# Layer 1's modulation vectors: from TensorE filler matmuls to VectorE sums inside the two-stream MLP

## The chip, the cores and the metric

One core of a Trainium2 chip runs the whole program. The metric is the device time of one execution in microseconds (us), the median of several executions. The engines are TensorE (PE), VectorE (DVE), ScalarE (ACT), GpSimd (POOL) and SyncE (SP, which issues nearly all DMA transfers here). The profile comes from one profiled execution.

## The reference, cut to what matters

A 256 x 1024 fp32 tensor passes through a first block (a hybrid layer and a recurrent layer, each with a squared-ReLU MLP) and then a second block of two layers on two streams, the tokens `xl` and a context `xc`. In each of its two layers, six modulation vectors per stream shift, scale and gate the normalised activations:

```python
def modulation(cvec, w_mod, b_mod):
    m = jax.nn.silu(cvec) @ w_mod + b_mod
    return jnp.split(m[:, None, :], N_MOD, axis=-1)      # N_MOD = 6

for i in range(DEPTH):                                   # DEPTH = 2
    ml = modulation(c, w_mod[i], b_mod[i])
    mc = modulation(c_ctx[None, :], w_mod[i], b_mod[i])
    hl = modulate(rmsnorm(xl, g_pre_mix[i]), ml[0], ml[1])
    hc = modulate(rmsnorm(xc, g_pre_mix[i]), mc[0], mc[1])
    ...
    xl_new = xl + ml[2] * rmsnorm(y_l, g_post_mix[i])
    h2 = modulate(rmsnorm(xl_new, g_pre_mlp[i]), ml[3], ml[4])
    xl_new = xl_new + ml[5] * rmsnorm(sqrelu_mlp_2(h2, w_mlp_in[i], w_mlp_out[i]), g_post_mlp[i])
```

`w_mod[i]` is 1024 x 6144 in fp32, 24 MB a layer, and both streams' vectors come from the same product, of a 2 x 1024 matrix with it. The vectors depend on `c` and `c_ctx` alone, so they can be made at any time before their layer uses them.

## The kernel before, in words

Order of the program, with the times of the trace: the hybrid layer (to 216 us), its MLP (to 402), the recurrent layer (to 515), its MLP (to 695), the second block's layer 0 on both streams (to about 950), the MLP of both streams, `mlp512` (to 1294), layer 1 (to 1440), and the last MLP. Nearly all matmuls hold fp32 accuracy by a split of each operand into a high and a low part. A weight unit of 1 MB is loaded into one of two buffers `wr`; ACT casts each half to `wh` (L407) and DVE subtracts to get `wl` (L408), four buffers each; every product is then three matmuls (high by high, high by low, low by high, L342). `pa`, `pb`, `pc` and `pm` are PSUM tiles: four banks, two, one and one.

The modulation vectors are made by the generator `mods()`: 48 steps, 24 for each of the two layers of the second block. A layer's 24 are three groups q of eight steps k. A step takes two tiles `wm` of 512 KB (four buffers, loaded on SP's queue at L737) and issues four fp32 matmuls (L776): the stationary operand is `cs_t[:, k, :]`, 32 columns of which two are used, the moving one 512 columns of `wm`, and the four write the four groups of 32 columns of one bank `pm`, a sum over k. After the eighth step DVE adds the bias and applies the gains (L782, L783), and `cols_of` turns the result by four transposes into `pc`, which DVE copies to `mc` (L755). Each matmul appears in the trace as two records.

What sets their place: calls `fill(n)` in the other stages take steps from the generator, and a scheduler fixes the order of the instructions on each engine ahead of the run; `tc.high_priority(-10)` marks these matmuls as to be placed late, as filler. The steps of layer 0 end at about 402 us. Those of layer 1 lie at 402 to 478, 694 to 780, 949 to 953 and 1299 to 1350 us.

In `mlp512` a unit of the first weight makes 256 hidden columns for each of the streams (`up`, into `pb`, squared ReLU by ACT and DVE at L560 and L1937), a unit of the second one is summed into four tiles of outputs (`acc`, into `pa`, added by DVE at L1948). Two `up` units and two `acc` units alternate. The last of the steps (two calls, j >= 14) were asked for here.

Of the kernel before, what the change touches and what calls it, by code (L numbers as in the profile page):

```python
# [10 lines left out]
F32 = mybir.dt.float32  # L11
# [4 lines left out]
P = 128  # L16
# [1 line left out]
SM = 1.0 / math.sqrt(96.0)  # L18
NW = 4
LEAD = 96  # L20
TRAIL = 24
ALPHA = 4.0 ** 0.25

ADD, SUB, MUL, MAX, MIN, POW = ALU.add, ALU.subtract, ALU.mult, ALU.max, ALU.min, ALU.pow
# [269 lines left out]
def hybrid_then_mla(ctx: ExitStack, tc: tile.TileContext, a, out, usizes):  # L294
    nc = tc.nc
# [18 lines left out]
    def s4(shape, dt=F32):  # L314
        return tmp.tile(shape, dt, tag="s4", bufs=5, name=nm("s4"))
# [19 lines left out]
    def psM():  # L335
        return psp.tile([P, 512], F32, tag="pm", bufs=1, name=nm("pm"))
# [4 lines left out]
    def mm(o, l, r, start, stop):  # L341
        T.matmul(o, l, r, start=start, stop=stop)  # L342
# [99 lines left out]
    half = cpool.tile([P, 8], F32, name="half")  # L442
    V.memset(half, -0.5)

    def row(name, n=1024, o=0):
        r = tmp.tile([P, 1024], F32, tag="row", bufs=3, name=nm("row"))
        i = ROWS.index(name)
        nc.sync.dma_start(out=r[:, :n], in_=a["rows"][i : i + 1, o : o + n].to_broadcast([P, n]))
        return r
# [273 lines left out]
        V.tensor_tensor(c2, c2, th, op=MUL)  # L723

    class WM:
        tiles, n = {}, 0

    def mod_load():

        if WM.n >= 48:  # L730
            return
        i, q, k = WM.n // 24, WM.n // 8 % 3, WM.n % 8
        for j in range(2):
            wm = wpool.tile([P, 2, 512], F32, tag="wm", bufs=4, name=nm("wm"))
            if WM.n < 2:
                G.tensor_copy(wm[:, 0, 0:1], WM.after)
            nc.sync.dma_start(out=wm, in_=a["wm"][i, q, k, j].rearrange("p (a b) -> p a b", a=2))  # L737
            WM.tiles[WM.n, j] = wm
        WM.n += 1

    mc = cpool.tile([P, 2, 3, 32], F32, name="mc")
    cpool.tile([P, TRAIL], F32, name="trail")

# [5 lines left out]
    def mods():  # L749

        def cols_of(m, i, q):
            pt = psC()
            for c in range(4):
                tr(pt[:, 128 * c : 128 * c + 128], m[:, 128 * c : 128 * c + 128])
            V.tensor_copy(mc[:, i, q].rearrange("p (c r s) -> p c r s", c=4, r=4),  # L755
                          pt.rearrange("p (c r s) -> p c r s", c=4, r=4)[:, :, :, 0:2])

        todo = None
        for n in range(48):
            i, q, k = n // 24, n // 8 % 3, n % 8  # L760
            if k == 0:
                ps = psM()
            if k == 1 and todo:
                cols_of(*todo)
            if k == 4:
                bg = s4([P, 2, 512])
                for r in range(4):
                    nc.sync.dma_start(
                        out=bg[32 * r : 32 * r + 32],
                        in_=a["bg"][i, q, r : r + 1].rearrange("o (a b) -> o a b", a=2).to_broadcast([32, 2, 512]),  # L770
                    )
            while WM.n < min(n + 2, 48):
                mod_load()
            for r in range(4):
                with tc.high_priority(-10):
                    mm(ps[32 * r : 32 * r + 32, :], cs_t[:, k, :], WM.tiles[n, r // 2][:, r % 2, :], k == 0, k == 7)  # L776
            mod_load()
            if k < 7:
                yield
                continue  # L780
            m = s2([P, 512])
            V.tensor_tensor(m, ps, bg[:, 0, :], op=ADD)  # L782
            V.scalar_tensor_tensor(m, m, K("one")[:, q : q + 1], bg[:, 1, :], op0=ADD, op1=MUL)  # L783
            for r in range(4):
                if 2 * q + r // 2 in (2, 5):
                    nc.sync.dma_start(
                        out=mdr[i, :, 2 * q + r // 2, 512 * (r % 2) : 512 * (r % 2) + 512], in_=m[32 * r : 32 * r + 2]
                    )
            todo = (m, i, q)
            yield  # L790
        cols_of(*todo)
        yield

    mod_g = mods()

    def fill(n):
        _take(mod_g, n)

    def run(g):
        for _ in g:  # L800
# [1065 lines left out]
    def layer1(xs, Ts, late):  # L1866

        m = Mixer(1)
        m.Ts = Ts
        w = (w_next(8), w_next(8))  # L1870
        fill(2)
        run(conf_inputs(m, w, 0))
        cg = conf_conv(m)
        late(0)
        w = (w_next(4), w_next(4))
        x0, x1 = latents(m, 1, 0, w), latents(m, 1, 1, w)
        _take(x0, 2)
        _take(x1, 2)
        _take(cg, 1)
        run(x0)  # L1880
        late(1)
        c0, c1 = latents(m, 0, 0, w, 160), latents(m, 0, 1, w, 160)
        _take(c0, 2)
        run(x1)
        fill(1)
        _take(cg, 1)
        _take(c1, 2)
        run(c0)
        run(c1)
        fill(1)  # L1890
        del m.Ts[0]
        gbr = row("g_branch1")
        cgb = row("conf1", 512)
        wq, wk = w_next(2), w_next(1)
        run(chain(queries(m, 1, wq), keys_values(m, 0, wk), keys_values(m, 1, wk)))
        m.qkT.clear()
        sc = short_conv(m)
        side = zipped(cg, sc, 2)
        at = attend(m, 1, 0)
        _pace(at, side, 1)  # L1900
        run(side)
        mc = lambda t: merge_conv(m, 1, t, gbr, cgb)
        ma = lambda t: merge_attn(m, 1, t, gbr)
        side = pipelined(mc(0), mc(1), ma(0))
        at = attend(m, 1, 1)
        _take(at, 2)
        _pace(at, side, 1)
        run(side)
        run(ma(1))
        fill(99)  # L1910
        GP = mrow(1, 0, 2)
        nT = Late()

        def done(t, halves):
            post_norm(xs[1][t], halves, GP)
            y = normed(xs[1][t])
            nT.fn[t] = lambda: to_xT(y, t, nT.xT, mod=(1, 1, 4))

        tm1024(m.mT[1], done, nT, (2, 3, 0, 1))
        return nT  # L1920

    def mlp512(Ts, xs, late):
# [27 lines left out]
        for kind, j in _mlp_order_512():  # L1950
            if kind == "w1":
                if j == 0:
                    w = (w_next(8), w_next(8))
                    q = {}
                    for i in range(2):
                        hid[i] = b8([P, 2, 2, 512], F32R)

                    def hid_tr(n):
                        p3 = head_tr(q[n])
                        sl = (slice(None), slice(None), slice(128 * n, 128 * n + 128))  # L1960
                        for i in range(2):
                            split(p3[:, 2 * i : 2 * i + 2], hid[i][:, 0][sl], hid[i][:, 1][sl])

                    before = None
                    for n in (2, 3, 0, 1):
                        late(n)
                        q[n] = square_relu(head(Ts[n // 2], n % 2, w))
                        if before is not None:
                            hid_tr(before)
                        before = n  # L1970
                elif j > 1:
                    w = w_next(8)
                    for s in (1, 0):
                        up(j, w, s)
                        if j == 2 and s:
                            hid_tr(1)
                    if j >= 14:
                        fill(1)
            elif j < 7:
                for c in range(2):  # L1980
                    w = w_next(4)
                    for n in range(4):
                        acc(j, c, w, n)
                del hid[2 * j], hid[2 * j + 1]
            else:
                GP = [mrow(0, 1, 5), mrow(0, 0, 5)]
                wa, wb = w_next(4), w_next(4)
                T1 = {1: new_xT()}
                fn = {}

                def ready(n):
                    if n in fn:
                        fn.pop(n)()

                def done(n):
                    s, t = n // 2, n % 2
                    y = yacc[n]
                    post_norm(xs[s][t], [y[:, 0:512], y[:, 512:1024]], GP[s])
                    z = normed(xs[s][t])

                    def go():
                        if s not in T1:
                            T1[s] = new_xT()
                        to_xT(z, t, T1[s], mod=(1, s, 1))

                    fn[n] = go

                for n in (2, 3):
                    acc(j, 0, wa, n)
                    acc(j, 1, wb, n)  # L2010
                    done(n)
                acc(j, 0, wa, 0)
                acc(j, 1, wb, 0)
                ready(2)
                acc(j, 0, wa, 1)
                ready(3)
                acc(j, 1, wb, 1)
                done(0)
                done(1)
# [47 lines left out]
```

## Time and profile before

| | us |
|---|---|
| median of 3 executions | 1632.86 (1632.76 to 1634.14) |
| the profiled execution | 1635.88 |
| its span in the trace | 1633.8 |
| PE busy | 1578.0 (97%) |
| DVE busy | 1029.0 (63%) |
| ACT busy | 743.3 (45%) |
| all `pm` matmuls of modulation, busy | 83.2 |

The span is 2.1 us short of the profiled execution's time, and that execution is 3.0 us above the median. A busy share is an average over stages with different limits: where an engine is busy all the time, an instruction added to it costs its full duration, and where it waits for others, an instruction removed from it may give nothing.

### The profile page before, as it was taken

How to read it: one execution, taken by the hardware profiler on the slowest of the kernel's cores; microseconds unless marked ns; L12 is line 12 of the kernel's file. 1: busy time of each engine (PE TensorE's matmuls, PEld its weight loads, DVE VectorE, ACT ScalarE, POOL GpSimd, SP SyncE). 2: the span in 40 equal slices, each digit the busy share in tenths (PEclk: the TensorE clock that was granted, in tenths of full speed). 3: DMA queues.
4: the chain of work that ended last, by engine and by line, in shares of the span. 5: the costliest groups of instructions: out<-in, count | busy, mean ns of one | idle time of the engine just before them, and what ended most of it. 6: DMA issues, size and time to landing. Idle time of an engine off the chain costs nothing.

```text
span 1633.8 us, 24905 instructions
## 1 busy us (share of the span) xinstructions
PE 1578.0 (97%) x10182; PEld 1358.9 (83%) x10182; DVE 1029.0 (63%) x1593; ACT 743.3 (45%) x1264; POOL 94.8 (6%) x121
## 2 busy tenths in 40 slices
PE   7999999999999999999999999999999999989998
PEld 7866679888878998877877789999999788779997
DVE  6874575556787556768974753444444789775555
ACT  5642244443574445436454543222222475554443
POOL 0021000000000000003010100000000030000000
PEclk9999999999999999999999999999999999989999
DMA  7865475555665554562310432222232262235553
GB/s 289 288 217 172 167 258 196 204 207 191 248 258 181 194 192 169 181 227 80 130 52 27 138 134 89 93 103 85 97 104 79 100 216 107 73 126 201 181 186 124
DMA packets 46946, 259.77 MB, mean 159 GB/s; under 512 B 5600, under 2 KB 5856, under 8 KB 24304
## 3 DMA queue, kind: packets, MB, share of 16 engines
q1 hardware_dynamic: 46832, 258.18, 44.9%
q8 instruction: 80, 1.31, 0.3%
q14 instruction: 34, 0.28, 0.1%
HBM read 257.08 MB, written 1.08 MB: 158 GB/s over the span
## 4 chain that ended last, share of the span: by engine, by line
PE 78%; DVE 8%; ACT 4%; DMA 2%; POOL 1%; issue 1%; POOLq 0%; DVEq 0%; ACTq 0%; SPq 0%
PE pa L342 44%; PE pb L342 27%; PE pm L342 4%; PE pb L366 2%; DVE wl L408 1%; DMA wr<-in_wp_dram 1%; PE pc L366 1%; ACT s L1389 1%; ACT wh L407 1%; DVE s L1583 1%; POOL ti L1395 1%; ACT s L1652 0%; DVE s L645 0%; DVE b L711 0%; DVE xt L1426 0%
## 5 line engine op out<-in xcount | busy, mean ns | idle before, releaser
L408 DVE TENSOR_TENSOR wl<-wr,wh 128x1024 fp32r<-128x1024 f32 (+2 forms) x366 | 443.4, 1217 | 301.4 <-ACT wh L407 288.4
L407 ACT CAST wh<-wr 128x1024 fp32r<-128x1024 f32 (+2 forms) x364 | 376.1, 1041 | 405.8 <-PE pa L342 202.6
L342 PE MATMUL pa<-wh,b 128*128 128x512 f32 (+3 forms) x1456 | 411.1, 365 | 12.5 <-ACT b L816 5.7
L342 PE MATMUL pb<-b,wh 128*128 128x256 f32 x2240 | 406.2, 284 | 0.0
L342 PEld LDWEIGHTS pb<-b,wh 128*128 128x128 f32 x2240 | 352.7, 192 | 7.2 <-issue 3.4
L342 PE MATMUL pb<-b,wl 128*128 128x256 f32 x1120 | 317.8, 284 | 0.0
L342 PEld LDWEIGHTS pa<-wh,b 128*128 128x128 f32 x1456 | 267.6, 195 | 57.1 <-ACT b L648 6.1
L342 PE MATMUL pa<-wl,b 128*128 128x512 f32 (+3 forms) x728 | 258.7, 364 | 8.9 <-DVE wl L408 8.9
L342 PE MATMUL pa<-wh,s 128*128 128x512 f32 x768 | 244.5, 391 | 0.0
L342 PEld LDWEIGHTS pb<-b,wl 128*128 128x128 f32 x1120 | 215.1, 192 | 1.7 <-issue 1.7
L342 PE MATMUL pa<-b,wh 128*128 128x256 f32 x1056 | 199.2, 289 | 3.7 <-ACT wh L407 1.9
L342 PEld LDWEIGHTS pa<-b,wh 128*128 128x128 f32 x1056 | 166.2, 193 | 16.0 <-issue 4.4
L342 PEld LDWEIGHTS pa<-wl,b 128*128 128x128 f32 x728 | 142.3, 195 | 35.3 <-DVE wl L408 13.5
L342 PEld LDWEIGHTS pa<-wh,s 128*128 128x128 f32 x768 | 144.4, 188 | 28.9
L342 PE MATMUL pa<-b,wl 128*128 128x256 f32 x528 | 150.1, 288 | 1.3 <-DVE wl L408 1.3
L342 PE MATMUL pa<-wl,s 128*128 128x512 f32 x384 | 150.4, 392 | 0.0
L342 PEld LDWEIGHTS pa<-b,wl 128*128 128x128 f32 x528 | 101.6, 193 | 8.2 <-DVE wl L408 3.3
L560 DVE TENSOR_TENSOR s<-s 128x512 f32<-128x512 f32 x80 | 54.9, 687 | 50.2 <-ACT s L558 50.2
L342 PE MATMUL pm<-wm,cs_t 128*32 128x512 f32 x384 | 83.2, 606 | 1.9 <-DMA wm<-in_wm_dram 1.7
L342 PEld LDWEIGHTS pa<-wl,s 128*128 128x128 f32 x384 | 72.3, 188 | 14.5 <-DVE wl L408 1.2
L1583 DVE SCALAR_TENSOR_TENSOR s<-cu,cols_sb,s 128x512 f32<-128x512 f32 (+1 forms) x120 | 70.7, 621 | 0.5
L366 PE MATMUL pb<-kc_sb,s 128*128 128x128 f32 x366 | 56.8, 279 | 10.8 <-DVE s L1408 2.5
(278 smaller groups left out, 1391.6 us busy)
## 6 DMA issues: line engine op xcount, KB each, us to landing
wr<-in_wp_dram SPq DMA_DIRECT2D x176, 1024.0 KB, 4.8
wm<-in_wm_dram SPq DMA_DIRECT2D x96, 512.0 KB, 5.2
row<-in_rows_dram SPq DMA_DIRECT2D x10, 512.0 KB, 5.5
wr<-in_wp_dram SPq DMA_DIRECT2D x4, 832.0 KB
s<-in_bg_dram SPq DMA_DIRECT2D x24, 128.0 KB, 5.6
row<-mdr SPq DMA_DIRECT2D x6, 512.0 KB, 3.5
wr<-in_wp_dram SPq DMA_DIRECT2D x4, 264.0 KB, 3.6
b<-in_xT_dram SPq DMA_DIRECT2D x4, 256.0 KB, 6.1
```

The costliest lines, as they stand in the source:

```text
L342: T.matmul(o, l, r, start=start, stop=stop)
L366: T.transpose(o, i, ident)
L407: S.copy(h[:, :n], r)
L408: V.tensor_tensor(l[:, :n], r, f(h[:, :n]), op=SUB)
L560: V.tensor_tensor(q, r, r, op=MUL)
L1389: S.activation(j, x, AF.Square, scale=scale, accum_out=o)
L1395: G.tensor_tensor(r, e, half[:, :1], op=POW)
L1583: V.scalar_tensor_tensor(ac, src, w(k), ac, op0=MUL, op1=ADD)
```

## The change

The steps of layer 0 stay in place. For layer 1, DVE takes over the sum over k: for each of three q and two halves j, two tiles `acc[0]` and `acc[1]` of 128 x 1024 (one for each stream; they take the three `row` buffers) collect `wm * c` over eight k, the first by TENSOR_SCALAR (L819), the seven others by SCALAR_TENSOR_TENSOR (L821), with the scalar a column of `cs_t`. What is left is a sum over the 128 partitions, which PE does with a stationary tile `sel` that has ones in one column and zeros in the rest: four matmuls for each (q, j), two column groups of `pm` with two matmuls each. Together that is 96 DVE operations (12 and 84) and 24 matmuls in place of the 96 matmuls of layer 1. Bias, gains and `cols_of` follow for each q. A new `fill1()` takes these units: after each `up` with j > 2, and after every second `acc` of the units with e < 7, all in `mlp512`. `fill` stops at the end of layer 0's steps. The loads of `wm` for layer 1 move along on SP's queue.

```diff
@@ mods(), layer 1
+        for q in range(3):
+            ps = psM()
+            for j in range(2):
+                acc = [row_tile() for _ in range(2)]
+                for k in range(8):
+                    n = 48 + 16 * q + 8 * j + k
+                    mod_load(n + 3)
+                    w = WM.tiles.pop((1, q, k, j)).rearrange("p a b -> p (a b)")
+                    for s_ in range(2):
+                        c = cs_t[:, k, s_ : s_ + 1]
+                        with tc.high_priority(-10):
+                            if k == 0:
+                                V.tensor_scalar(acc[s_], w, c, None, op0=MUL)
+                            else:
+                                V.scalar_tensor_tensor(acc[s_], w, c, acc[s_], op0=MUL, op1=ADD)
+                    mod_load(n + 4)
+                    yield
+                for r in (2 * j, 2 * j + 1):
+                    with tc.high_priority(-10):
+                        for s_ in range(2):
+                            mm(ps[32 * r : 32 * r + 32, :], sel[:, s_, :], acc[s_][:, 512 * (r % 2) : 512 * (r % 2) + 512], s_ == 0, s_ == 1)
+            cols_of(*biased(ps, gains(1, q), 1, q))
+            yield
@@ mlp512
                     for s in (1, 0):
                         up(j, w, s)
+                        if j > 2:
+                            fill1()
...
-                    if j >= 14:
-                        fill(1)
...
                     for n in range(4):
                         acc(j, c, w, n)
+                        if n % 2:
+                            fill1()
```

On PE, where the first products of the second block's layer 0 begin after the recurrent layer's MLP (about 698 us), the order before has this run of filler. `b`, `wh` and `wl` are operands of the products, the `pc` row is the transposes of `cols_of`:

```order
L342 MATMUL pa_6621<-b_572_6024,wh_6553 128x256
L342 MATMUL pa_6621<-b_573_6025,wh_6553 128x256
L342 MATMUL pm_6673<-wm_5820,cs_t 32x512
L342 MATMUL pm_6673<-wm_5822,cs_t 32x512 x2
L342 MATMUL pm_6673<-wm_6198,cs_t 32x512 x2
L342 MATMUL pm_6673<-wm_6200,cs_t 32x512 x2
L366 MATMUL pc_6682<-kc_sb,s_596_6202 128x128 x4
L342 MATMUL pm_6673<-wm_6678,cs_t 32x512 x2
L342 MATMUL pm_6673<-wm_6680,cs_t 32x512 x2
L342 MATMUL pa_6571<-b_572_6024,wl_6550 128x256
```

In the order of the change the `pm` rows and the four `pc` transposes of `cols_of` are gone from here, and the `pa` rows follow each other.

On PE inside an `acc` unit of `mlp512`, where there was no `pm` row before, the change has six such groups of four matmuls. The first, the third and the fifth look like this (`row_9231` and `row_9232` are the two streams' sums):

```order
L342 MATMUL pa_9647<-wh_9601,b_1057_9351 128x512
L342 MATMUL pm_9230<-row_9231,sel 32x512
L342 MATMUL pa_9647<-wh_9601,b_1057_9351 128x512
L342 MATMUL pm_9230<-row_9232,sel 32x512
L342 MATMUL pm_9230<-row_9231,sel 32x512
L342 MATMUL pa_9647<-wl_9602,b_1057_9351 128x512
L342 MATMUL pm_9230<-row_9232,sel 32x512
L342 MATMUL pa_9647<-wh_9601,b_1057_9351 128x512
```

The second has one `pa` row after its first row, the fourth and the sixth are four rows together; all now stand between products that had followed each other without a break.

On DVE at the passage from layer 0 to `mlp512`, the order before has, from the second residual tile `xt_90` to its normalisation:

```order
L1426 SCALAR_TENSOR_TENSOR xt_90<-s_1004_8724,ti_8730,xt_90 128x512
L1394 SCALAR_TENSOR_TENSOR ti_8740<-ti_8736 128x1
L1408 TENSOR_SCALAR s_1009_8737<-xt_90,ti_8741 128x512 x2
L408 TENSOR_TENSOR wl_8598<-wr_8591,wh_8597 128x1024
L645 TENSOR_SCALAR s_1016_8785<-pb_8780,mc 128x128 x3
```

and the change has (its lines are 44 numbers further down, so L1470 is L1426, L1438 is L1394, L1452 is L1408):

```order
L1470 SCALAR_TENSOR_TENSOR xt_90<-s_972_8603,ti_8609,xt_90 128x512
L819 TENSOR_SCALAR row_9232<-wm_3048,cs_t 128x1024
L821 SCALAR_TENSOR_TENSOR row_9232<-wm_3050,cs_t,row_9232 128x1024
L1438 SCALAR_TENSOR_TENSOR ti_8619<-ti_8615 128x1
L408 TENSOR_TENSOR wl_8490<-wr_8483,wh_8489 128x1024
L1452 TENSOR_SCALAR s_977_8616<-xt_90,ti_8620 128x512 x2
L408 TENSOR_TENSOR wl_8780<-wr_8483,wh_8779 128x1024
```

Two of the sums, and a `wl`, have moved ahead of the normalisation.

## Rows read from the trace of the kernel before

**Rows 1.** The page, its span, busy time of engines, chain by line

```profile
span 1633.8 us, 24905 instructions
...
PE 1578.0 (97%) x10182; PEld 1358.9 (83%) x10182; DVE 1029.0 (63%) x1593; ACT 743.3 (45%) x1264; POOL 94.8 (6%) x121
...
PE pa L342 44%; PE pb L342 27%; PE pm L342 4%; PE pb L366 2%; DVE wl L408 1%; DMA wr<-in_wp_dram 1%; PE pc L366 1%; ACT s L1389 1%; ACT wh L407 1%; DVE s L1583 1%; POOL ti L1395 1%; ACT s L1652 0%; DVE s L645 0%; DVE b L711 0%; DVE xt L1426 0%
```

**Rows 2.** Windows by stage: PE, PEld, DVE, ACT, POOL busy, clock, DMA share, GB/s

```profile
402.00:480.00 78.00, 75.63 (x573) 63.62 (x572) 63.90 (x99) 51.57 (x85) 0.92 (x1) 1.00 0.65 242
...
1090.00:1140.00 50.00, 50.00 (x333) 46.24 (x333) 22.13 (x26) 15.57 (x19) 0.00 (x0) 1.00 0.25 85
...
1290.00:1350.00 60.00, 55.24 (x376) 44.89 (x374) 53.44 (x116) 41.17 (x88) 16.82 (x24) 1.00 0.52 178
```

**Rows 3.** Windows, instructions of tile pm alone: PE, PEld, DVE busy, clock, DMA, GB/s

```profile
402.00:480.00 78.00, 12.26 (x64) 1.96 (x64) 0.00 (x0) 1.00 0.65 242
694.00:780.00 86.00, 12.87 (x64) 2.11 (x64) 0.00 (x0) 0.98 0.43 154
...
sum 224.00, PE 36.30 PEld 5.91 DVE 0.00; mean PE 9.07 PEld 1.48 DVE 0.00
```

**Rows 4.** Chain of waits, 400 to 412 us: start, duration, what, records

```profile
by line: PE pa L342 50.1%; PE pm L342 39.7%; PE pc L366 8.5%; PE pb L366 3.6%
...
402.07 1.83 PE pm L342 x10
...
404.81 0.97 PE pm L342 x2
```

**Rows 5.** Chain of waits, 694 to 722 us

```profile
by line: PE pa L342 57.0%; DMA wm<-in_wm_dram 15.1%; PE pm L342 11.0%; DVE s L645 3.8%; PE pb L366 3.7%; ACT b L648 2.2%; DVE cu L1537 2.1%; ACT s L647 1.7%; PE pc L366 1.6%; SPq L737 1.0%; issue 0.9%; ACTq L647 0.1%
...
699.54 4.22 DMA wm<-in_wm_dram
...
703.80 1.05 PE pm L342 x4
```

**Rows 6.** Timeline of DVE at 410, 702 and 894 us: start, busy, what [idle before]

```profile
410.44 0.19 DVE L755 COPY mc<-pc 128x32 f32<-128x32 f32 x1 [1.89 <-PE pc L366]
...
701.63 1.17 DVE L408 TENSOR_TENSOR wl<-wr,wh 128x1024 fp32r<-128x1024 f32 x1
...
894.17 0.69 DVE L1421 TENSOR_TENSOR s<-s,row 128x512 f32<-128x512 f32 x1 [8.43 <-ACT s L1828]
```

**Rows 7.** Chain of waits, 432 to 484 us

```profile
by line: DMA wr<-in_wp_dram 22.2%; DVE wl L408 16.0%; DVE b L1365 9.1%; issue 6.5%; PE pa L342 4.9%; DVE b L1363 4.7%; DVE b L711 4.5%; ACT wh L407 4.1%; ACT b L1360 3.9%; DVE b L1269 3.5%; DVE b L1357 3.5%; ACT L1360 2.5%; DVE s L1319 2.4%
```

**Rows 8.** Chain of waits, 750 to 782 us

```profile
by line: PE pa L342 27.8%; issue 14.9%; ACT b L1498 9.2%; PE pm L342 8.8%; DVE b L1608 6.6%; DVE s L1607 6.5%; POOL s L1484 3.7%; ACT b L1621 3.6%; ACT b L1620 3.6%; ACT s L1603 3.4%; ACT s L1627 3.4%; ACT b L1496 2.7%; POOL ti L1467 2.1%; 
```

**Rows 9.** Chain of waits, 947 to 954 us

```profile
by line: PE pm L342 40.3%; PE pa L342 33.5%; PE pb L366 20.9%; PE pc L366 6.2%
```

**Rows 10.** Chain of waits, 1296 to 1352 us

```profile
by line: PE pa L342 37.5%; DMA wr<-in_wp_dram 11.1%; PE pm L342 8.8%; DVE wl L408 5.4%; ACT wh L407 4.9%; ACT s L1389 4.0%; DVE s L645 3.1%; PE pb L366 2.9%; issue 2.8%; POOL s L1484 2.8%; POOL ti L1395 2.2%; PE pc L366 2.0%; POOL ti L1467 
...
1332.64 0.99 PE pm L342 x8
```

**Rows 11.** DVE groups, from the page and from the answer on line 1408

```profile
L408 DVE TENSOR_TENSOR wl<-wr,wh 128x1024 fp32r<-128x1024 f32 (+2 forms) x366 | 443.4, 1217 | 301.4 <-ACT wh L407 288.4
...
L1583 DVE SCALAR_TENSOR_TENSOR s<-cu,cols_sb,s 128x512 f32<-128x512 f32 (+1 forms) x120 | 70.7, 621 | 0.5
...
L1408 DVE TENSOR_SCALAR s<-xt,ti x16: 479/484/489, 696.2 to 1445.5; 128x512 f32<-128x512 f32 x16
```

**Rows 12.** Windows, PE alone: busy, clock, DMA share, GB/s

```profile
506.00:510.00 4.00, 1.62 (x14) 1.00 0.10 16
510.00:514.00 4.00, 4.00 (x24) 0.58 0.92 358
...
702.00:706.00 4.00, 3.25 (x18) 1.00 1.03 412
```

More of the change, by code (lines that the diff above doesn't have):

```diff
@@ L20 @@
 LEAD = 96
-TRAIL = 24
+TRAIL = 88
 ALPHA = 4.0 ** 0.25
@@ L443, in hybrid_then_mla, with row_tile @@
     V.memset(half, -0.5)
+    def row_tile():
+        return tmp.tile([P, 1024], F32, tag="row", bufs=3, name=nm("row"))
     def row(name, n=1024, o=0):
@@ L725, in hybrid_then_mla, with mod_load @@
     class WM:
[L726 to L733, printed above, removed]
+        tiles, n, first = {}, 0, False
+        order = [(0, q, k, j) for q in range(3) for k in range(8) for j in range(2)]
+        order += [(1, q, k, j) for q in range(3) for j in range(2) for k in range(8)]
+    def mod_load(upto):
+        for n in range(WM.n, min(upto, len(WM.order))):
+            at = WM.order[n]
             wm = wpool.tile([P, 2, 512], F32, tag="wm", bufs=4, name=nm("wm"))
-            if WM.n < 2:
+            if n < 4:
                 G.tensor_copy(wm[:, 0, 0:1], WM.after)
-            nc.sync.dma_start(out=wm, in_=a["wm"][i, q, k, j].rearrange("p (a b) -> p a b", a=2))
-            WM.tiles[WM.n, j] = wm
-        WM.n += 1
+            nc.sync.dma_start(out=wm, in_=a["wm"][at].rearrange("p (a b) -> p a b", a=2))
+            WM.tiles[at] = wm
+            WM.n = n + 1
+    sel = cpool.tile([P, 2, 32], F32, name="sel")
+    V.memset(sel, 0.0)
+    for s_ in range(2):
+        V.memset(sel[:, s_, s_ : s_ + 1], 1.0)
     mc = cpool.tile([P, 2, 3, 32], F32, name="mc")
@@ L756, in cols_of, with gains, biased @@
                           pt.rearrange("p (c r s) -> p c r s", c=4, r=4)[:, :, :, 0:2])
[L758 to L773, printed above, removed]
-            for r in range(4):
[L775 to L780, printed above, removed]
+        def gains(i, q):
+            bg = s4([P, 2, 512])
+            for r in range(4):
+                nc.sync.dma_start(
+                    out=bg[32 * r : 32 * r + 32],
+                    in_=a["bg"][i, q, r : r + 1].rearrange("o (a b) -> o a b", a=2).to_broadcast([32, 2, 512]),
+                )
+            return bg
+        def biased(ps, bg, i, q):
             m = s2([P, 512])
@@ L788, in mods, with fill1 @@
                     )
-            todo = (m, i, q)
+            return m, i, q
+        todo = None
+        for n in range(24):
+            q, k = n // 8, n % 8
+            if k == 0:
+                ps = psM()
+            if k == 1 and todo:
+                cols_of(*todo)
+            if k == 4:
+                bg = gains(0, q)
+            mod_load(2 * n + 4)
+            for r in range(4):
+                with tc.high_priority(-10):
+                    mm(ps[32 * r : 32 * r + 32, :], cs_t[:, k, :], WM.tiles[0, q, k, r // 2][:, r % 2, :], k == 0, k == 7)
+            mod_load(2 * n + 6)
+            if k < 7:
+                yield
+                continue
+            todo = biased(ps, bg, 0, q)
             yield
         cols_of(*todo)
-        yield
+        yield "first"
+        for q in range(3):
+            ps = psM()
+            for j in range(2):
[7 more added lines that the diff above has]
+                        with tc.high_priority(-10):
+                            if k == 0:
+                                V.tensor_scalar(acc[s_], w, c, None, op0=MUL)
[4 more added lines that the diff above has]
+                for r in (2 * j, 2 * j + 1):
+                    with tc.high_priority(-10):
+                        for s_ in range(2):
+                            mm(ps[32 * r : 32 * r + 32, :], sel[:, s_, :], acc[s_][:, 512 * (r % 2) : 512 * (r % 2) + 512], s_ == 0, s_ == 1)
+            cols_of(*biased(ps, gains(1, q), 1, q))
+            yield
     mod_g = mods()
     def fill(n):
-        _take(mod_g, n)
+        for _ in range(n):
+            if not WM.first:
+                WM.first = next(mod_g) == "first"
+    def fill1():
+        next(mod_g, None)
     def run(g):
@@ L1909, in layer1 @@
         run(ma(1))
-        fill(99)
+        assert next(mod_g, None) is None
         GP = mrow(1, 0, 2)
```

## The prediction

> **What bounds the kernel now.** I read the page first: PE is busy 97% of the span and holds most of the chain that ended last, pa and pb products alone 71%, while DVE is busy 63% [rows 1]. That invites the change: take work from PE, give it to DVE. But the share is an average, so I read the windows by stage next. In the two-stream MLP PE is busy 50.00 of 50 us and DVE only 22.13; just after it, from 1290 to 1350 us, DVE is busy 53.44 of 60 and PE 55.24 [rows 2]. What is added to PE inside the MLP has nothing to lie beside. Then I read where layer 1's modulation matmuls lie: the tile pm alone takes 12.26 us of 402 to 480 and 12.87 of 694 to 780, and the four stretches that hold all 24 steps give 36.30 us together [rows 3]. Last I read the chain of waits through these stretches, to see which of that time ends anything.
>
> The chain's shares, times the lengths of their windows, say what pm is worth there at the most. 400 to 412 us: 39.7% of 12, 4.8 us [rows 4]. 432 to 484 us: no share at all; weights' DMA, wl and the recurrence on DVE fill the chain [rows 7]. 694 to 722 us: 11.0% of 28, 3.1 us, and another 4.2 us in which PE waited for a wm transfer [rows 5]. 750 to 782 us: 8.8% of 32, 2.8 us [rows 8]. 947 to 954 us: 40.3% of 7, 2.8 us [rows 9]. 1296 to 1352 us: 8.8% of 56, 4.9 us [rows 10]. Sum: 22.6 us of the 36.3. That is a ceiling for the gain, since behind each piece another wait stands ready.
>
> **What is removed, stretch by stretch.**
> - 400 to 412 us. The pms hold up four transposes on PE, and DVE's copy from pc had waited 1.89 us for them [rows 6]; the normalisation behind the copy carries the chain on. Beyond that the next products wait for ACT's split. I take 1.9 us, ends 0 and 4.8.
> - 432 to 484 us. The pms fill holes that DVE, ACT and the DMA make [rows 7]. The wr transfers are 22.2% of 52 us, 11.5 us, and share the queues with wm; these loads go. I take 0.75 us, ends 0 and 3.
> - 694 to 722 us. The wait for wm and the pm behind it end at 703.80 + 1.05 = 704.85 us [rows 5]. The next product needs a wl that DVE finishes at 701.63 + 1.17 = 702.80 [rows 6]. So 2.0 us, ends 0 and 7.3, and PE then idles where it had filler.
> - 750 to 782 us. ACT, DVE and POOL hold the rest of that chain [rows 8] and will be late next. I take 1.2 us, ends 0 and 2.8.
> - 947 to 954 us. 2.8 us of pm go, but DVE gets new work in the passage before it: the order puts a TENSOR_SCALAR and a SCALAR_TENSOR_TENSOR of 128x1024, by the prices below 2.2 us, ahead of the normalisation of the second tile, on which transposes and then products wait. The four sums that are put earlier fall in a hole of 8.43 us on DVE [rows 6] and cost nothing; without that hole they would be some 5 us. I take a net gain of 0.5, ends 2.8 and a loss of 1.5.
> - 1296 to 1352 us. DVE is busy 89% there [rows 2] and its convolution paces the stretch, so of 4.9 us I take 0.75, ends 0 and 4.9.
>
> Sum of gains 1.9 + 0.75 + 2.0 + 1.2 + 0.5 + 0.75 = 7.1 us.
>
> **What the holes cost.** Where the filler goes, PE idles some us. From 506 to 510 us PE was busy 1.62 us of 4, and in the next 4 us its mean granted clock was 0.58, full speed being 2.4 GHz and the lower level half of it: 0.42 x 4 = 1.7 us lost. From 702 to 706 us, with a shorter hole, it stayed at 1.00 [rows 12]. New holes come at about 410, 700 and 1300 us. I take 2.0 us, a little over one such loss; ends 0 and 5.1 for three.
>
> **What is added to PE.** Twenty-four matmuls with 32 columns out and 512 in, in six groups of four, all inside products that keep PE at 50 of 50 us. Such a matmul alone (two records) takes 0.97 us of PE; a whole step of four, one for each column group, takes 0.99 (eight records) [rows 4, 10]; and ten records, a step and one matmul more, take 1.83 [rows 4]. So different column groups run side by side and a second matmul for the same group takes another 0.85 or so. A group of the change is s0, s1 of one column group, then s0, s1 of the next: the two middle ones can pair, so three rounds, 0.97 + 0.86 + 0.86 = 2.7 us where the four stand together, and 3 x 0.97 = 2.9 where products stand between them. Six of them: about 2.8 x 6 = 16.9 us. Lower end two rounds, 1.83 x 6 = 11.0; upper end no pairing, 4 x 0.97 x 6 = 23.3. The trace has no two matmuls of one column group that follow each other directly with others waiting, so I keep both ends.
>
> A page speaks of this: the Trainium skill, TensorEngine Tiling (Array Packing), section Theoretical Speedup, gives up to four times for operands of at most 32 columns, from independent 128x32 tiles. By it two column groups would run fully in parallel, which is the lower end, and the sum below would be 5.9 us smaller; the step of four in 0.99 us agrees with it, and no row shows it for two matmuls queued on each of two groups.
>
> Layer 1's three cols_of, of four transposes each, now stand in the full stretch too. Two sets of transposes hold 8.5% of 12 us of the chain from 400 us, 1.0 us [rows 4], so three are 1.5; they cost something where they stood before, and I take 1.3, ends 0 and 1.5.
>
> **What is added to DVE.** Twelve TENSOR_SCALAR and 84 SCALAR_TENSOR_TENSOR of 128x1024, neither in the trace at this size. Twice the 128x512 forms, 0.484 and 0.621 us [rows 11], is 0.97 and 1.24; L408, as large, takes 1.22. So 12 x 0.97 + 84 x 1.24 = 116 us over some 310 us, 37 points on top of 44% [rows 2]: 81%. DVE stays short of full; sums wait where wl and the y additions go first. I price it at 0 here, because wl is made ahead into four buffers, up to about 10 us where that cover fails. The loads, 24 MB over 310 us, add 77 GB/s to the 85 of rows 2, below the 242 of the window from 402 [rows 2]. Nothing.
>
> **Sum.** 16.9 + 1.3 + 2.0 - 7.1 = +13.1 us on a span of 1633.8. The median is 1632.86 and the profiled run 3.0 us above it; I put the difference on the median: 1646.0 us.
>
> **Rivals.**
> - *The removed time pays* (faster). If behind the chain's pm pieces nothing stands ready, the full 22.6 us return and the holes close. Then 16.9 + 1.3 - 22.6 = -4.4: 1628.5 us. For it: the chain names these pieces. Against: the 1.89 us of row 410.44 and the wl at 702.80 show the next wait within 2 us [rows 6]. It decides when the stretches at 400, 694 and 1296 shorten by over half of their chain pm. 18%.
> - *Half and half.* Gains near 13 us with two rounds, 11.0 + 1.3 - 13 = -0.7, about 1632: no change to be measured. 7%.
> - *Two rounds* instead of three, rest as forecast: 13.1 - 5.9 = +7.2, 1640. 10%.
> - *The clock drops in every new hole.* Five holes (400, 434, 700, 716, 1300 us) at 1.7 instead of 2.0 in all: +6.5, 1652.5 us. For it: the window after 510 us [rows 12]; against: that after 702. 8%. The Trainium skill, TensorE: Matmul & The Clock Gate, section What's actually happening, says that the throttled state is the default and activity releases it, which is this mechanism; the window at 702 us shows a hole without it.
> - *DVE turns late in the MLP.* A sum stands in front of a wl or a y addition, or waits for its wm, and PE idles in a stretch that never idled: 10 us more, 1656. 81% busy on average can be full for a while. 7%.
> - The forecast itself: 50%, by itself 1639 to 1654 us.
>
> **How the numbers follow.** About 0.2%, 3.3 us, is what a measurement of this kernel tells from no change. Slower: forecast, two rounds, clock and DVE, 75%. Same: half and half, 7%. Faster: 18%. The range takes the bounds of the matmuls' price (1640 to 1652) and reaches down to 1629 so that only half of the faster case is left out, and up to 1657.
>
> **What would show it.** In the changed profile the MLP stage should be about 18 us longer, with pm and pc on the chain there and PE still full; the matmuls from `row` and `sel` should take about 2.8 us a group; DVE near 80% there. The stretches before should be shorter by 2 to 7 us, with new idle time on PE, ended by DVE or ACT, where pm lay, and lower clock behind some. The forecast is wrong if layer 0 and the recurrent layer shorten by over 12 us, if a group takes under 2 us, or if PE idles in the MLP.

## The result and the profile after

The changed kernel takes 1651.82 us in the median (1651.12 to 1653.99), the kernel before 1633.06 beside it: ratio 1.0116, interval 1.0098 to 1.0133. It is 18.8 us slower; 13.1 us were forecast.

The page of the changed kernel, its span, busy times, chain by line, and the group of the new sums:

```profile
span 1649.0 us, 24740 instructions
...
PE 1570.9 (95%) x10038; PEld 1358.6 (82%) x10038; DVE 1136.9 (69%) x1692; ACT 743.7 (45%) x1264; POOL 95.4 (6%) x121
...
PE pa L342 42%; PE pb L342 27%; PE pm L342 3%; PE pb L366 2%; DVE wl L408 2%; DVE s L1627 1%; POOL ti L1439 1%; PE pc L366 1%; ACT wh L407 1%; DVE s L648 1%; ACT s L1433 1%; ACT s L1696 0%; DVE b L714 0%; DVE s L1452 0%; DVE xt L663 0%
...
L821 DVE SCALAR_TENSOR_TENSOR row<-wm,cs_t,row 128x1024 f32<-128x1024 f32 x84 | 105.6, 1280 | 0.5
```

Against [rows 1], DVE gained 108 us and PE lost only 7 us, though 96 matmuls went and 24 came. A lower PE share in a longer span: PE waits more than it did.

To see where the time went, I follow the start of the same instruction in both traces. Before, from the chain of waits and from the timelines (ACT's casts and PE's first `up` product of the two-stream MLP):

```profile
704.85 10.39 PE pa L342 x85
715.25 0.45 PE pb L366 x4
...
896.67 9.55 PE pa L342 x40
...
1296.18 0.66 PE pc L366 x4
```

```profile
399.24 1.06 ACT L407 CAST wh<-wr 128x1024 fp32r<-128x1024 f32 x1 [8.03 <-PE pa L342]
...
490.04 2.00 ACT L407 CAST wh<-wr 128x1024 fp32r<-128x1024 f32 x2 [1.54 <-PE pa L342]
...
958.96 0.40 PE L342 MATMUL pb<-b,wh 128*128 128x256 f32 x2
...
1363.93 2.09 ACT L407 CAST wh<-wr 128x1024 fp32r<-128x1024 f32 x2
```

After, the same instructions in the same views:

```profile
695.28 12.25 PE pa L342 x85
707.53 0.45 PE pb L366 x4
...
890.17 9.55 PE pa L342 x40
...
1311.17 0.66 PE pc L366 x4
```

```profile
394.94 2.00 ACT L407 CAST wh<-wr 128x1024 fp32r<-128x1024 f32 x2 [8.03 <-PE pa L342]
...
482.63 2.00 ACT L407 CAST wh<-wr 128x1024 fp32r<-128x1024 f32 x2 [2.16 <-PE pa L342]
...
954.43 0.40 PE L342 MATMUL pb<-b,wh 128*128 128x256 f32 x2
...
1377.17 1.04 ACT L407 CAST wh<-wr 128x1024 fp32r<-128x1024 f32 x1
```

| up to | start before | start after | shift | change of shift |
|---|---|---|---|---|
| end of the hybrid layer's MLP | 399.24 | 394.94 | -4.3 | |
| end of the recurrent layer | 490.04 | 482.63 | -7.4 | -3.1 |
| layer 0's 85 products, first | 704.85 | 695.28 | -9.6 | -2.2 |
| the transposes behind them | 715.25 | 707.53 | -7.7 | +1.9 |
| last products of layer 0 | 896.67 | 890.17 | -6.5 | +1.2 |
| first `up` of the MLP | 958.96 | 954.43 | -4.5 | +2.0 |
| transposes behind the MLP | 1296.18 | 1311.17 | +15.0 | +19.5 |
| layer 1, a cast | 1363.93 | 1377.17 | +13.2 | -1.8 |
| end of the span | 1633.8 | 1649.0 | +15.2 | +2.0 |

The 4.3 us of the first line come ahead of anything that the change touches (in the eleven other traces that cast starts between 396.3 and 398.2 us). The two profiled executions lie 3.0 us above and 0.7 us below their medians, which nearly accounts for the difference between +15.2 in the spans and +18.8 in the medians. Behind the first line, the MLP alone lost 19.5 us, and all stages outside it, from which 36 us of matmuls went, came out even: -3.1 - 2.2 + 1.9 + 1.2 + 2.0 - 1.8 + 2.0 = 0.

In the MLP, before and after (window 993 to 1290; PE, PEld, DVE, ACT, POOL busy, clock, DMA share, GB/s):

```profile
993.00:1290.00 297.00, 297.00 (x1900) 271.60 (x1899) 138.58 (x171) 89.60 (x119) 1.96 (x3) 1.00 0.27 93
```

```profile
993.00:1290.00 297.00, 297.00 (x1855) 257.83 (x1854) 212.70 (x233) 82.17 (x101) 0.00 (x0) 1.00 0.47 161
```

PE is busy without a break in both. DVE went from 47% to 72%, with no wait of PE on it in this window. What lengthened the stage is on PE itself. The chain of waits of the changed kernel in two of the six groups:

```profile
1019.14 0.98 PE pm L342 x2
1020.12 0.42 PE pa L342
1020.55 0.98 PE pm L342 x4
1021.53 0.42 PE pa L342
1021.95 0.98 PE pm L342 x2
1022.93 7.25 PE pa L342 x31
...
1167.85 1.85 PE pm L342 x8
...
1173.59 0.44 PE pc L366 x4
```

A split group takes three pieces of 0.98, and the lone product between two of them 0.42, where a product in a run takes 7.25 / 31 = 0.23. A group that stands together takes 1.85. The cols_of adds 0.44.

Outside, the granted clock of PE in the changed kernel (busy, clock, DMA share, GB/s):

```profile
692.00:696.00 4.00, 0.72 (x3) 0.57 0.00 0
696.00:700.00 4.00, 4.00 (x23) 0.58 0.86 266
...
944.00:948.00 4.00, 2.53 (x13) 0.64 0.30 120
948.00:952.00 4.00, 4.00 (x21) 0.51 0.15 29
```

The 85 products begin 2.2 us earlier than before, as their hole was emptied, then start at the lower clock (0.58 from 696 to 700 us) and take 12.25 us instead of 10.39. The last products ahead of the MLP, at 944 to 952 us, are at the lower clock too.

### The profile page after: what moved, and what is told of

Same layout as the page of the kernel before. It is cut to its first block, busy times and chain, and to the rows that moved or that the text cites. A ratio compares the mean times of both kernels' runs of the same rounds, so it can differ in the third digit from the quotient of the medians.

```text
span 1649.0 us, 24740 instructions
## 1 busy us (share of the span) xinstructions
PE 1570.9 (95%) x10038; PEld 1358.6 (82%) x10038; DVE 1136.9 (69%) x1692; ACT 743.7 (45%) x1264; POOL 95.4 (6%) x121
## 4 chain that ended last, share of the span: by engine, by line
PE 76%; DVE 11%; ACT 5%; issue 2%; POOL 2%; DMA 0%; POOLq 0%; DVEq 0%; ACTq 0%
PE pa L342 42%; PE pb L342 27%; PE pm L342 3%; PE pb L366 2%; DVE wl L408 2%; DVE s L1627 1%; POOL ti L1439 1%; PE pc L366 1%; ACT wh L407 1%; DVE s L648 1%; ACT s L1433 1%; ACT s L1696 0%; DVE b L714 0%; DVE s L1452 0%; DVE xt L663 0%
## 5 line engine op out<-in xcount | busy, mean ns | idle before, releaser
L342 PE MATMUL pa<-b,wh 128*128 128x256 f32 x1056 | 200.3, 290 | 11.8 <-ACT b L651 5.1
L342 PEld LDWEIGHTS pa<-b,wl 128*128 128x128 f32 x528 | 101.8, 194 | 11.8 <-DVE wl L408 10.3
L821 DVE SCALAR_TENSOR_TENSOR row<-wm,cs_t,row 128x1024 f32<-128x1024 f32 x84 | 105.6, 1280 | 0.5
L1439 POOL TENSOR_TENSOR ti<-ti,half 128x1 f32<-128x1 f32 x26 | 23.9, 920 | 785.5 <-DVE ti L1438 785.5
```

What stands on the lines that cost most here:

```text
L821: V.scalar_tensor_tensor(acc[s_], w, c, acc[s_], op0=MUL, op1=ADD)
L1439: G.tensor_tensor(r, e, half[:, :1], op=POW)
```

## Experiments

**Only the removal.** From the changed kernel, layer 1's loop of `mods()` is left out, and both layers take the same vectors.

```diff
-        for q in range(3):
-            ps = psM()
-            for j in range(2):
...
-            cols_of(*biased(ps, gains(1, q), 1, q))
-            yield
```

> Layer 1's steps are left out altogether: no matmuls, no VectorE sums, no loads for them; layer 1 uses the vectors of layer 0. So this is the change's removal without its additions. Theory A (the removed filler lay in holes, and where it did hold something up, the next wait or the lower clock takes most of it back): 3 us gained at 402 to 410 us, near 0 at 694 to 722, at most 3 us in all elsewhere, so 1628 to 1633 us against 1633 before, and the 85 products after the hole at 700 us take about 12.2 us as in the changed kernel, not 10.4. Theory B (what the chain of waits names is what can be gained): 22 us faster, near 1610 us.

Measured 1632.18 us, ratio 0.9982 (0.9969 to 0.9995); run again it gave 1632.88, ratio 0.9991 (0.9982 to 1.0000). The medians of the kernel before beside them were 1634.18 and 1634.20. So the removal of all 24 steps is worth 1.3 to 2.0 us, not the 22.6 of the chain (of which 4.2 were a wait for a transfer). The MLP's length, first `up` to the transposes behind it, is 337.1 us as before (337.2). The chain of waits shows the products after the hole slow again:

```profile
698.61 12.11 PE pa L342 x85
```

**Most of the partition sums left out**, all VectorE sums kept.

```diff
-                for r in (2 * j, 2 * j + 1):
-                    with tc.high_priority(-10):
-                        for s_ in range(2):
-                            mm(ps[32 * r : 32 * r + 32, :], sel[:, s_, :], acc[s_][:, 512 * (r % 2) : 512 * (r % 2) + 512], s_ == 0, s_ == 1)
+                if j:
+                    with tc.high_priority(-10):
+                        mm(ps, ident, acc[0][:, 0:512], True, True)
```

> As the change, with all its VectorE sums and loads, but one 128x512 matmul for each q in place of the eight with 32 columns, so most of the partition sums are left out. Theory A (the two-stream MLP grew by 19.6 us because TensorE there has no free time, and VectorE's sums cost nothing): the MLP grows by 5 to 7 us instead of 19.6, total near 1638 us. Theory B (VectorE at 70 to 80% busy delays what TensorE waits for): the MLP still grows by over 10 us, total over 1643 us.

Measured 1637.08 us, ratio 1.0013 (1.0000 to 1.0025); the MLP takes 341.3 us, 4.1 more than before, less than I expected. Theory A stands: the matmuls left out cost the MLP 15 of its 19.5 us, and DVE's 84 + 12 operations at the most a part of the 4.1 that stayed, in which three matmuls and the three `cols_of` (3 x 0.44) still lie.

**The eight matmuls of a q together.** Four row buffers, neighbours in different column groups, no late priority.

```diff
-                for r in (2 * j, 2 * j + 1):
-                    with tc.high_priority(-10):
...
+                accs[j] = acc
+            for s_ in range(2):
+                for r in range(4):
+                    mm(ps[32 * r : 32 * r + 32, :], sel[:, s_, :], accs[r // 2][s_][:, 512 * (r % 2) : 512 * (r % 2) + 512], s_ == 0, s_ == 1)
```

> As the change, but the sums of both halves are kept (four row buffers instead of three) and the eight matmuls of a q are issued together, neighbours in different column groups, without the late priority: three runs of eight instead of six groups of four, three of which were split by products. Theory A (the MLP's growth is the column time of these matmuls plus what each break in the products costs): eight matmuls in four column groups take two rounds, 1.85 us, each cols_of 0.44, each break some 0.3, so the MLP grows by 3 x 2.6 = 8 us instead of 19.6, total 1639 to 1642 us. Theory B (the growth comes from VectorE's sums and their waits): it stays near 1652 us.

Measured 1644.11 us, ratio 1.0060 (1.0037 to 1.0084). PE's timeline has sixteen records, a whole q, in the time that eight took (1164.47 to 1166.33):

```profile
1164.47 1.92 PE L342 MATMUL pm<-row,sel 128*32 128x512 f32 x16
```

The MLP takes 344.9 us, 7.7 more than before, where 8 was expected. The total, 9.4 us above the kernel before in the same runs, was expected 2 us lower; 1.7 us of it lie outside the MLP. Three things were changed at once here, so the 11.8 us that the MLP won back can only be shared out by the pieces read above: standing together saves 15.3 - 6 x 1.85 = 4.2 us (15.3 is what the six groups took, worked out below), four column groups in place of two another 6 x 1.85 - 3 x 1.85 = 5.5, and fewer breaks among the products about 2. The split groups were less than half of it.

**The sums held back** until the first output tile of the MLP (their first loads wait for it).

```diff
+            if n < 4 or 48 <= n < 52:
                 G.tensor_copy(wm[:, 0, 0:1], WM.after)
...
+                        if j == c == n == 0:
+                            WM.after = yacc[0][:, 0:1]
```

> As the change, but the loads of layer 1's first four tiles wait for the first output tile of the two-stream MLP, so that no sum can move ahead of it on VectorE. Theory A (the sums that stand ahead of the normalisations between layer 0 and the MLP cost there, 2 us directly and up to 2.8 us by the lower clock after the holes that they make): the passage is 2 to 5 us shorter, total 1647 to 1650 us. Theory B (the passage lost its time by the removal of the filler alone): no change there, total near 1652 us.

Measured 1651.56 us, ratio 1.0104 (1.0089 to 1.0119). From layer 0's last products to the first `up` it takes 955.46 - 893.21 = 62.2 us; the changed kernel takes 954.43 - 890.17 = 64.3, the kernel before 62.3. The passage is 2.0 us shorter, as theory A has it, and the chain of the changed kernel names the sums that moved ahead, before normalisations:

```profile
929.38 1.19 DVE row L821
```

But that the sums themselves cost these 2.0 us does not follow. The next experiment leaves all sums where the changed kernel has them, and its passage begins at the same time (890.20 us) and has the same PE busy times up to 948 us. There the clock stayed at 1.00:

```profile
944.00:948.00 4.00, 2.53 (x19) 1.00 0.30 119
948.00:952.00 4.00, 4.00 (x36) 1.00 0.13 13
```

Its first `up` starts at 951.98 us, 2.45 earlier than in the changed kernel, and its passage takes 61.8 us, 0.5 less than before. So in these traces the loss came with the low clock at 944 to 952 us, and the sums without it cost nothing. With the sums held back the clock was low for a shorter time there: 1.00 from 944 to 948 us and 0.61 from 948 to 952. The total gained only 0.3 us here, less than the runs can tell. With the removal alone the passage takes 62.2 us.

**Filler put back in one hole.** Four steps of matmuls whose results nobody reads, where layer 1's steps lay at 694 to 705 us.

```diff
+    def dummy(n, hp):
+        for _ in range(n):
+            ps = psM()
+            for r in range(4):
+                with tc.high_priority(-10):
+                    mm(v3(ps[32 * r : 32 * r + 32, :], 2), cs_t[:, 0, :], f(hp[:, 0:2, 0:256]), True, True)
...
-        fill(2)
+        dummy(4, w[1].parts[0][0])
         late.ready(0)
```

> As the change, plus four steps of filler matmuls (results unused) in the hole of 4.7 us that TensorE has before layer 0's products, where layer 1's steps lay before. Theory A (the 2 us gained there were given back by the lower clock after the hole): the hole is filled, the granted clock stays at 1.00 there, the 85 products take 10.4 us instead of 12.25, and the kernel is about 1.9 us shorter from there on, near 1650 us. Theory B (something else slows these products, such as their weights): they take about 12 us as in the changed kernel, time unchanged.

Measured 1653.24 us, ratio 1.0112 (1.0095 to 1.0128). Windows of PE, then the chain of waits:

```profile
692.00:696.00 4.00, 3.74 (x32) 1.00 0.00 0
...
708.00:712.00 4.00, 1.49 (x12) 0.95 0.00 0
712.00:716.00 4.00, 4.00 (x24) 0.62 0.00 0
```

```profile
697.32 10.45 PE pa L342 x85
```

At the place theory A is shown: with the hole filled the clock stays at 1.00 and the 85 products take 10.45 us. For the total it failed: the four executions took 1650.12 to 1654.59 us. In the profiled one, the shortest, the clock was at 0.62 behind the next hole, at 712 us, where the changed kernel had 1.00, and at 0.72 from 744 to 748 us (1.00), and it was at 1.00 from 944 to 952 us. Whether the filler moved the low stretches, or they would have fallen elsewhere in another execution anyway, one trace can't tell.

**Removal with holes filled**, seven, two and two such steps at about 694, 924 and 1297 us; beside it the removal alone, unchanged, once more.

```diff
-        fill(2)
+        dummy(7, w[1].parts[0][0])
         late.ready(0)
...
-        fill(2)
+        dummy(2, w[0].parts[0][0])
         run(conf_inputs(m, w, 0))
...
                     w = (w_next(8), w_next(8))
+                    dummy(2, w[0].parts[0][0])
                     q = {}
```

> As the run that leaves layer 1's steps out, plus eleven steps of filler matmuls (results unused, operands already on the chip) meant for the holes of TensorE: seven for those at 694 and 711 us, two at 924 us, two at 1297 us. Theory A (the lower clock after these holes eats what the removal gains): the granted clock stays at 1.00 there, 3 to 5 us faster than without the filler, 1627 to 1629 us. Theory B (the next waits eat it, and the low clock only falls on other stretches): within 2 us of the run without the filler, 1630 to 1633 us.

> The run that leaves layer 1's steps out, once more, on the same chip as the run with its holes filled: 1631 to 1633 us, about 2 us faster than the kernel before; a ratio of 1.000 or more would take back the 2 us.

Measured 1630.88 us with, 1632.88 without filler (the ratio for the first 0.9986, 0.9976 to 0.9996), 2.0 us apart: between the two theories. Windows of PE with and without:

```profile
696.00:700.00 4.00, 3.82 (x31) 1.00 0.07 19
...
748.00:752.00 4.00, 3.37 (x16) 0.50 0.99 369
...
928.00:932.00 4.00, 3.79 (x33) 1.00 0.78 305
948.00:952.00 4.00, 4.00 (x22) 0.57 0.00 0
...
1300.00:1304.00 4.00, 3.30 (x26) 1.00 0.19 40
```

```profile
696.00:700.00 4.00, 0.77 (x3) 0.53 0.00 0
...
748.00:752.00 4.00, 2.67 (x21) 1.00 0.86 276
...
928.00:932.00 4.00, 4.00 (x22) 0.57 0.80 272
948.00:952.00 4.00, 2.98 (x22) 1.00 0.00 0
...
1300.00:1304.00 4.00, 3.79 (x17) 0.57 0.13 22
```

At the three filled holes the low stretches went, and others came at 748 and 948 us. The intervals of the two kernels overlap, so a gain from filling is likely here but not shown, and the 3 to 5 us of theory A did not come. The eleven executions with filler fall in two groups: six at 1630.0 to 1630.9 us with a mean clock of 0.988 to 0.990, five at 1633.3 to 1634.5 us with 0.985 to 0.987. So time goes with the clock, and the clock differs between executions of one and the same kernel.

**No filler at 402 to 410 us.** The kernel before, with the first loads of layer 1's steps waiting for a later tile.

```diff
+            if WM.n in (24, 25):
+                G.tensor_copy(wm[:, 0, 0:1], WM.hold)
...
-        if not last:
-            fill(2)
...
+        WM.hold = at[:, 0, 0:1]
+        fill(2)
```

> The kernel before, all of it on TensorE, with one difference: layer 1's first steps can't be issued at 402 to 410 us, since their tiles' loads wait for the first output of the recurrent layer's gate (about 436 us). Theory A (of all the filler only that at 402 to 410 us held the chain, 3 us): 3 us gained at 410 us; kept if the steps fit the holes after 436 us, total 1630 to 1631 us. Theory B (the loads and matmuls bunched after 436 us hold the weights' transfers or the recurrence there): up to 3 us lost again by 500 us, total 1633 or above.

> As the run before, with the loads waiting for the first chunk of the recurrent layer's convolution (about 415 us), so that the transfers are spread more and the last steps of q 0 stand in the holes at 478 to 500 us. Theory A: 3 us gained at 410 us and some of the holes at 478 to 500 us filled, so no low clock there: 1629 to 1631 us. Theory B: steps stand among products at 415 to 434 us, where TensorE is full, and cost 1 us each: 1632 to 1634 us.

Measured 1636.34 us, ratio 1.0013 (1.0002 to 1.0024), and, with `cT[0]` in place of `at`, 1634.81, ratio 0.9997 (0.9983 to 1.0010). Neither gained anything, as theory B has it. In the second the gain is there at first: from the cast at the end of the hybrid layer's MLP to the end of the next layer's first 20 products it takes 15.8 us (before 18.4, after the change 15.8). By the end of the recurrent layer it is gone (91.4 us from that cast, before 90.8, after the change 87.7): the 3 us do not stay won once the work has to lie somewhere else.

**The last hole of the kernel before filled.** The kernel before has a hole of 4.1 us ahead of the first products of its last MLP; `dummy` is the function shown above. Its windows there, without filler:

```profile
1434.00:1438.00 4.00, 1.14 (x10) 1.00 0.13 16
1438.00:1442.00 4.00, 2.72 (x12) 0.55 0.62 246
```

```diff
         w = (w_next(8), w_next(8))
+        dummy(steps, w[0].parts[0][0])
...
         hid_tr(q0, 0)
+        dummy(steps // 3, w[0].parts[0][0])
...
-    mlp256(T2, done)
+    mlp256(T2, done, steps=3)
```

> The kernel before, with four steps of filler matmuls (results unused) added at the start of the last MLP, three of them in TensorE's longest hole, 4.1 us at 1435 to 1439 us, after which the granted clock was 0.70 and 0.60 for some 6 us. Theory A (the lower clock costs what its stretch loses): the clock stays at 1.00 there, 2 to 3 us faster, ratio near 0.9985. Theory B (the products there wait for something else, or the low clock falls on the next hole): within 1 us of the kernel before.

```profile
1434.00:1438.00 4.00, 3.74 (x26) 1.00 0.41 119
1438.00:1442.00 4.00, 4.00 (x32) 1.00 0.34 143
```

Measured 1632.01 us against 1634.62, ratio 0.9988 (0.9978 to 0.9998): 2.6 us less than the kernel before in the medians, with an interval that only just leaves out no change. With the second `dummy` left out:

```diff
         hid_tr(q0, 0)
-        dummy(steps // 3, w[0].parts[0][0])
```

> The run with the last hole filled, with three steps of filler in place of four: the fourth had its first matmul at the hole's end and the other three among products, about 2 us of TensorE on the chain. Theory A (only what is past the hole costs): the clock still stays at 1.00, 1 to 2 us faster than with four steps, ratio to the kernel before 0.9975 to 0.9985. Theory B (with the hole filled less, the low clock comes back there or after the next hole at 1446 us): ratio 0.999 to 1.000.

Measured 1632.94 us against 1634.10, ratio 0.9993 (0.9983 to 1.0003). The clock stayed at 1.00 there too, as theory A has it, but the gain can't be told from none, as theory B has it; whether three or four steps are better stays open.

Up to that hole these two kernels and the kernel before have the same instructions in the same order on TensorE, VectorE, ScalarE and GpSimd, and still their low stretches lie at different places there. The kernel before, then the one with four steps:

```profile
700.00:704.00 4.00, 1.91 (x10) 1.00 0.97 339
```

```profile
700.00:704.00 4.00, 4.00 (x20) 0.66 1.04 422
```

At 860 to 864 us the kernel with three steps has 0.60 and the two others 1.00. So the order of the instructions alone does not fix where the low clock falls, and one low stretch more or less between two single traces does not show what an edit did. At 694 us there is more to go by: in all six traces of kernels that leave the hole empty the clock was low behind it, and the 85 products took 12.1 to 12.3 us.

## Why the prediction was right, and where it was off

The side, the size within the range and the place were right. The size owes something to luck: the range was 28 us wide, and the forecast was near in the MLP (18.2 for 19.5 us) because two errors in it went opposite ways, while outside the MLP the 5.1 us that were to be won did not come. Of its own signs of being wrong one came true: a group under 2 us, in two of the six. The stretches ahead of the MLP were to be 2 to 7 us shorter, and from the first line of the table on they were 0.2 us shorter.

- *The price in the MLP* was 16.9 + 1.3 = 18.2 us, and 19.5 came. Its parts were off in both directions. Split groups took 2.94 us as worked out (2.9). Those two that stand together took 1.85, the lower end, not 2.7: the two middle matmuls were not the only pair. All six took 3 x 2.94 + 2.82 + 2 x 1.85 = 15.3 us (the second group, with one product between, took 0.98 + 1.84). By the rule of the Trainium skill, TensorEngine Tiling (Array Packing), section Theoretical Speedup, the lower end was to be expected, and the measurement agrees with it for the groups that stand together: 1.85 for four and, in four column groups, 1.85 for eight. Unpriced were the breaks: 19.5 - 15.3 - 1.3 = 2.9 us are left. Seven lone products at 0.42 - 0.23 make 1.3 of it; that the rest is restarts of the products is argued, not measured.
- *DVE for nothing* was right: 72% busy in the MLP's window where 81% was expected, no wait of PE. The sums cost 1.28 us each (1.24 expected).
- *The removal*, 7.1 us of gains less 2.0 for the clock, was the step that failed: 5.1 us were to be gained, and nothing was (with the removal alone 1.3 to 2.0). From 402 to 484 us 3.1 came for 1.9 + 0.75. At 694 us the 2.0 came as worked out, 2.2, and 1.9 of it went again within the next 85 products. At 750 to 890 us 1.2 was lost where 1.2 was to be gained. In the passage 2.0 was lost for a gain of 0.5, with the low clock there; without it, in the run with the hole at 694 us filled, the 0.5 came. In layer 1 1.8 was gained and 2.0 lost behind it.
- *The clock* was mis-sized: 2.0 us. Two places alone show 1.9 us (the 85 products, 12.25 for 10.39) and 2.45 us (the passage). Over the span the mean granted clock is 0.986, before 0.991; (1 - 0.986) x 1649.0 - (1 - 0.991) x 1633.8 = 8.4 us more of full-clock time was withheld, an upper bound, since PE also idles in such stretches. The rival in which the clock drops in every new hole, 1652.5 us, had 8% and came nearest in the number, not in the mechanism: in the changed kernel the clock stayed at 1.00 behind new holes at 396 to 400, 428 to 432 and 708 to 712 us. Shown is the mechanism at 694 us: with the hole filled the 85 products took 10.45 us, with it empty 12.25 and 12.11. The Trainium skill, TensorE: Matmul & The Clock Gate, section What's actually happening, has activity release the throttle, and the filled hole agrees. The loss at 750 to 890 us is not the clock's: it was 1.00 from 700 to 944 us after the change. What it is stays open, as does the loss behind 1364 us.
- *The removed time pays* fell with the removal alone. The chain named pieces that the next wait, or the lower clock, replaced.

## What to carry to other kernels

Work that an engine does in its waiting time is not a saving when it goes: price it by the next release behind each piece, not by its share of the busy time or of the chain. What is left of it on the full engine should stand in one block, with neighbours in different column groups, and never be split by other products. And before filler on TensorE is taken out, look at the clock behind its hole: at 694 us it took back 1.9 of the 2.2 us that the emptied hole gave. Whether filler put in on purpose pays in the total is only hinted at here.

## What was not expected of the hardware

- A hole's low clock is not tied to the hole alone. Holes of 2.5 us at 708 to 712 us were followed by 1.00 in one kernel and by 0.62 in another, and kernels with the same instructions in the same order up to there had 1.00 and 0.66 at 700 to 704 us.
- With matmuls that nobody reads, in a hole of 4.1 us, the kernel before measured a ratio of 0.9988 (0.9978 to 0.9998), and with a quarter fewer 0.9993 (0.9983 to 1.0003).
- Four 32-column matmuls, two for each of two column groups, took 1.85 us when they stood together, and eight in four column groups took the same.
- A lone 128x512 product between two 32-column pieces took 0.42 us against 0.23 in a run.
- SCALAR_TENSOR_TENSOR on 128x1024 fp32 took 1.28 us, TENSOR_SCALAR 0.75.
